# A block of attention values in front of the x0 projections, in the first two quarters of a Hyena and neighbourhood-attention layer

## The chip, the cores and the metric

The kernel runs on one core of one Trainium2 chip. The metric is the time of one execution on the device in microseconds (us), as the median of several runs. The kernel is one program without loops at run time: every loop below is unrolled by Python when the program is written.

## The reference

The layer takes 640 tokens of width 1024: 128 prompt tokens and 512 latent tokens (an 8 x 64 grid). After an adaptive scale and shift, one wide projection gives everything else:

```
z = h @ w_in
hy, g_h, qkv, g_a, m = split(z)          # 3*1024, 1024, 3*1024, 1024, 2*1024
hy = short_conv(hy, conv_w, conv_b)      # three taps along the sequence
v_h, x1, x0 = split(hy)
u = v_h * x1
y_h = (irfft(rfft(u, 2L) * rfft(filter, 2L)) + u * d_bias) * x0
y_a = attention(q, k, v)                 # 8 x 16 window plus context keys for the latents
p_h = (y_h * silu(g_h)) @ w_bh ;  p_a = (y_a * silu(g_a)) @ w_ba
out = (sigmoid(m_h) * p_h + sigmoid(m_a) * p_a) @ w_out
x  <- layer_norm(alpha * x + gate * out)
```

The new keys and values of the prompt are outputs too. All of it is float32; the kernel splits each operand into a high and a low part and multiplies three times (high by high, high by low, low by high).

## The kernel before

**Layout.** Channels lie on the 128 partitions, so a projection of 128 channels for 640 tokens is one "tile": eight steps of the contraction, three passes, two halves of 320 tokens, which makes 48 matmuls into two PSUM banks (`proj`, `accumulate`, L178 to L197). Two pools of four banks each share PSUM: `ps_mm` (`acc`, tag "mm") for projections and values, `ps_ax` (`aux`) for the rest.

**The Hyena branch** works in four quarters of 256 channels, two channel tiles each. For quarter q:

- `quarter_head(q)` (L503) projects the tiles 2q, 8+2q, 2q+1 and 9+2q. Each goes through `conv_tile` (L477): four copies on ACT (L482 to L486) bring the tile from PSUM into one of two buffers `zs`, which take turns; ACT makes the middle tap (L488), and DVE adds the two outer taps (two L490). The first of a pair is called u, the second x1, and DVE multiplies them (L513). Four buffers "u" and two buffers "cv" (for x1) take turns.
- `quarter_tail(q)` (L527) does the same with the tiles 16+2q and 17+2q, which are x0 and lie in the ring "yh" of nine rows. It ends with `gate_convs(q)`.
- `long_conv`, `long_conv_product` and `long_conv_back` are the long convolution: transposes (L547) and a Fourier transform of u on PE, products with the filter's spectrum on DVE (L588, L589, L591, L596, L597), and the way back (PE L171 to L173 and L648). `filter_spectrum(q)` makes that spectrum (PE L391 to L402, DVE L407, the products `fa`, `fb`, `fc`, `fd`). At the end DVE adds the bias term into u (L640, L650).
- `gate_conv(n)` (L520) multiplies u by x0 (L472, L475) and stores the product in DRAM from POOL's queue (L524). It is called twice for each n, from the tail and from the way back; the second call does the work, and with it u and x0 are free.

**The attention values** are computed by `values(m)` (L656), each call for 256 columns, in token-major form: the tokens are the stationary operand and the weights stream. One call takes two weight tiles. For each half of the contraction it writes 48 matmuls on the first four token tiles into two banks `v` (L669), then 12 on the fifth token tile into a third bank `ve` (L680). With a home given, as here, the result goes through two "cv" buffers (L689, L690) and is stored in DRAM by five transfers from SP's queue (L691 to L694).

**Weights.** `wtile` (L150) loads a raw tile on SP's queue, writes its negative into `wl` (ACT, L162), has POOL's queue add the tile from DRAM (L163) after ACT has made `wh` its copy in fp32r's precision (L164); there are two raw, two `wh` and three `wl` buffers.

**The order.** `quarters()` (L1324) strings heads, tails and values together as the main line. `convs()` and `filters()` are a side line; they wait for flags such as `whole1` (head 1 written) or `spectrum1`. `weave` (L1348) takes three steps of the side line for every two of the main line, and every second main step also takes one of `token_sums`. This sets the order in which instructions are written. In this stage the order of execution is then made by the framework's planner, which gives each engine, among what is ready, the instruction that was written first, going by estimated times; on each engine the chosen order is fixed in the program. The attention stage from L1399 on has its order written by hand.

```
    weave(chain(along(quarters(), sums, 2), hand_over()), braid(convs(), filters()), AHEAD_OF[0], AHEAD_OF[1])
```

Of the kernel before, what the change touches and what calls it, by code (L numbers as in the profile page):

```python
# [46 lines left out]
def tile_hyena_natten_step(ctx: ExitStack, tc: tile.TileContext, a, o):  # L47
# [50 lines left out]
    def acc(name):  # L98
        return ps_mm.tile([P, 512], F32, tag="mm", name=name)
# [6 lines left out]
    def row(pool, tag, name, dt=F32, bufs=NK + 1, n=NT):  # L106
        return pool.tile([P, NT + 4 if tag == "yh" else NT], dt, tag=tag, bufs=bufs, name=name)[:, :n]
# [42 lines left out]
    def wtile(i, eng=None, dst=None, width=P):  # L150
        if i in early:
            return early.pop(i)
        if i not in raws:
            wraw(i)
        if dst is None:
            wh = wp.tile([P, 1024], F32R, tag="wh", name=f"wh{i}")
            wl = wp.tile([P, 1024], F32R, tag="wl", bufs=3, name=f"wl{i}")
            dst = [wh[:]], [wl[:]]
        raw, n = raws.pop(i), 1024 // len(dst[0])
        if eng == "dma":  # L160
            (wh,), (wl,) = dst
            nc.scalar.activation(wl, raw[:], AF.Copy, scale=-1.0)  # L162
            nc.gpsimd.dma_start(wl, a["wall"][i], accum_op=ALU.add)  # L163
            nc.scalar.activation(wh, raw[:], AF.Copy)  # L164
        else:
            for j, (wh, wl) in enumerate(zip(*dst)):
                split(wh, wl, raw[:, n * j : n * j + n], eng)
        return [[w[c // n][:, c % n : c % n + width] for c in range(0, 1024, width)] for w in dst]
# [308 lines left out]
    def conv_tile(i, dst):  # L477
        lo, hi = yield from proj(i, eng="dma")
        convw = out["convw"]
        zs = zss[0]  # L480
        zss.reverse()
        nc.scalar.activation(zs[:, 1 : 1 + LP], lo[:, :LP], AF.Copy)  # L482
        nat = by_row(zs[:, GAP + 1 : NG + 1])
        nc.scalar.activation(nat[:, :, 7:8], from_blocks(lo[:, B7], 1), AF.Copy)
        nc.scalar.activation(nat[:, :, 0:2], from_blocks(lo[:, B01], 2), AF.Copy)  # L485
        nc.scalar.activation(nat[:, :, 2:7], from_blocks(hi[:, :HALF], 5), AF.Copy)  # L486
        d = dst[:, :NG]
        nc.scalar.activation(d, zs[:, 1 : 1 + NG], AF.Identity, scale=convw[:, i, 1:2], bias=convw[:, i, 3:4])  # L488
        for c in (0, 2):
            nc.vector.scalar_tensor_tensor(d, zs[:, c : c + NG], convw[:, i, c : c + 1], d, op0=ALU.mult, op1=ALU.add)  # L490
# [12 lines left out]
    def quarter_head(q):  # L503
        us = []
        out[f"u{q}"] = us
        for i in range(2):
            n = 2 * q + i
            u = hw.tile([P, NG + 1], F32, tag="u", bufs=4, name=f"u{n}")
            x1 = hwa.tile([P, NG + 1], F32, tag="cv", bufs=2, name=f"x1_{n}")
            yield from conv_tile(n, u)  # L510
            yield
            yield from conv_tile(8 + n, x1)
            nc.vector.tensor_tensor(u[:, :NG], u[:, :NG], x1[:, :NG], op=ALU.mult)  # L513
            us.append(u)
            yield
        out[f"whole{q}"] = True
# [10 lines left out]
    def quarter_tail(q):  # L527
        for i in range(2):
            n = 2 * q + i
            out["x0"][n] = row(yhp, "yh", f"x0_{n}", n=NG + 1)  # L530
            yield from conv_tile(16 + n, out["x0"][n])
            yield
        if q < 3:
            gate_convs(q)

    def gate_convs(q):
        for i in range(2):
            gate_conv(2 * q + i)
# [117 lines left out]
    def values(m, home=None):  # L656
        w = [wtile(T_V + 2 * m + i, "dma", width=256) for i in range(2)]
        ps = [acc(f"v{m}_{i}") for i in range(2)]

        def passes(k):  # L660
            wh, wl = w[k // 4][0][k % 4], w[k // 4][1][k % 4]
            return ((hH, wh, k == 0, False), (hL, wh, False, False), (hH, wl, False, k == NK - 1))

        for half in range(2):
            ks = range(4 * half, 4 * half + 4)
            for k in ks:
                for x, wk, first, last in passes(k):
                    for t in range(4):
                        nc.tensor.matmul(  # L669
                            ps[t // 2][:, t % 2 * 256 : t % 2 * 256 + 256], x[:, k, P * t : P * t + P], wk,  # L670
                            start=first and t % 2 == 0, stop=last, skip_group_check=True,
                        )
                yield
            if half:
                parts = [ps[0][:], ps[1][:]]
            else:
                pe = acc(f"ve{m}")
            for k in ks:
                for x, wk, first, last in passes(k):
                    nc.tensor.matmul(pe[:, :256], x[:, k, P * 4 :], wk, start=first, stop=last, skip_group_check=True)  # L680
            yield
        if home is None:
            v = out[f"v{m}"] = slot(m, "v", f"v{m}")
            for c, p in ((0, parts[0]), (512, parts[1]), (1024, pe[:, :256])):
                nc.scalar.activation(v[:, c : c + p.shape[-1]], p, AF.Copy)
        else:
            for i, p in enumerate(parts):
                v = hwa.tile([P, NG + 1], F32, tag="cv", bufs=2, name=f"v{m}_{i}")
                nc.scalar.activation(v[:, :512], p, AF.Copy)  # L689
                nc.scalar.activation(v[:, 512:640], pe[:, 128 * i : 128 * i + 128], AF.Copy)  # L690
                nc.sync.dma_start(home[m][:, 512 * i : 512 * i + 512], v[:, :512])  # L691
                nc.sync.dma_start(home[m][:, 1024 + 128 * i : 1152 + 128 * i], v[:, 512:640])
                if i == 0:
                    nc.sync.dma_start(o["new_v"][:, m * 256 : m * 256 + 256], v[:, :256])  # L694
            yield
            return
        nc.sync.dma_start(o["new_v"][:, m * 256 : m * 256 + 256], v[:, :256])
        yield
# [61 lines left out]
    def chain(*gens):  # L760
        for g in gens:
            yield from g
# [28 lines left out]
    def slot(j, tag, name, dt=F32):  # L791
        pool = out["slots_l" if j % 2 == 0 else "slots_q" if tag[0] == "q" else "slots_r"]
        return pool.tile([P, SLOT[tag]], dt, tag=tag, name=name)
# [529 lines left out]

    def quarters():  # L1324
        for q in range(3):
            yield from chain(quarter_head(q + 1), quarter_tail(q))
            if q < 2:
                yield from values(2 + q, v_d)

    def convs():  # L1330
        yield from chain(until("whole0"), long_conv(0))
        for q in range(4):
            yield from chain(until(f"spectrum{q}"), long_conv_product(q))
            back = long_conv_back(q)
            while f"rows{q}" not in out:
                yield next(back)
            if q < 3:
                yield from until(f"whole{q + 1}")
            yield from braid(back, long_conv(q + 1) if q < 3 else iter(()))
        yield from chain(until("slots_q"), attention_setup())  # L1340
# [5 lines left out]

    sums = chain(token_sums(0), token_sums(1))
    weave(chain(along(quarters(), sums, 2), hand_over()), braid(convs(), filters()), AHEAD_OF[0], AHEAD_OF[1])  # L1348
    out["slots_r"] = left.enter_context(tc.tile_pool(name="slots_r", bufs=1, reuse_waits="tile"))
    pinned[0] = True  # L1350
# [384 lines left out]
```

## Time and profile before

| | |
|---|---|
| median of 3 runs | 883.93 us (883.04 to 885.12) |
| profiled execution | 883.7 us, its span 881.9 us |
| PE busy | 866.0 us, 98% of the span |
| DVE busy | 645.1 us, 73% |
| ACT busy | 450.2 us, 51% |
| POOL busy | 189.0 us, 21% |
| DMA | 168.82 MB, 191 GB/s on average |

PE is the matmul engine (TensorE), PEld its weight loads, DVE the vector engine, ACT the scalar engine, POOL GpSimd, SP the queue that issues most transfers. A timeline row gives the start, the duration, the engine, the line of the kernel, the instruction with its output and inputs by name (buffer numbers left out), and in brackets how long the engine had been idle before and what released it. Rows that are merged carry a count at their end. A busy PE overlaps its matmuls: the time that one adds is the distance between starts, not its duration.

By the timeline the stages are: the prologue to about 50 us; the four quarters with values(2) at 111 to 128 us, values(3) at 197 to 219 and values(1) and values(0) at 296 to 329; queries, keys and the first gates to 358; the attention stage to about 702; the merge and the output to the end.

### The profile page before, as it was taken

To read this page: it belongs to the slowest core of one execution; us is meant where nothing else is said; L and a number is where in the kernel's file an instruction comes from. 1 tells how busy PE (TensorE), PEld (TensorE's weight loads), DVE (VectorE), ACT (ScalarE), POOL (GpSimd) and SP (SyncE) were. 2 spreads that over 40 slices of the span, in tenths; PEclk is the share of its full clock that TensorE was granted. 3 is DMA by queue.
4 is the path that set the end of the run, shared out by engine and by line. 5 is a ranking of instruction groups with operands and counts; after the bars stand their busy time and mean duration, and the time that the engine had idled before them with its cause. 6 is when DMAs were issued, how large, how long until landed. Compare 5 with 4: busy or idle time off the path is not lost.

```text
span 881.9 us, 17167 instructions
## 1 busy us (share of the span) xinstructions
PE 866.0 (98%) x6464; PEld 836.8 (95%) x6464; DVE 645.1 (73%) x1229; ACT 450.2 (51%) x960; POOL 189.0 (21%) x216
## 2 busy tenths in 40 slices
PE   8999999989999999999999999999999999999996
PEld 7899999979999999999999999999999999999885
DVE  4778986596895852787867787677778488667666
ACT  4396555546446453566566556656666532243200
POOL 0012210100100112084353334333454200000000
PEclk9999999989999999999999999999999999999999
DMA  8978886435664799978776668675854587445521
GB/s 326 400 170 226 231 215 145 92 103 138 162 132 96 202 228 241 308 218 252 172 238 164 220 153 260 138 212 158 232 138 120 180 301 246 160 165 187 183 88 56
DMA packets 75822, 168.82 MB, mean 191 GB/s; under 512 B 11067, under 2 KB 29243, under 8 KB 75740
## 3 DMA queue, kind: packets, MB, share of 16 engines
q1 hardware_dynamic: 56492, 123.32, 41.9%
q0 software_dynamic: 13632, 38.80, 22.8%
q10 hardware_dynamic: 5616, 5.61, 1.9%
q8 instruction: 51, 0.84, 0.4%
q14 instruction: 31, 0.25, 0.1%
HBM read 143.06 MB, written 23.99 MB: 189 GB/s over the span
## 4 chain that ended last, share of the span: by engine, by line
PE 94%; DVE 3%; DMA 1%; ACT 1%; issue 1%; SPq 0%; POOL 0%; POOLq 0%; DVEq 0%; ACTq 0%
PE mm L183 33%; PE sp L1238 30%; PE out L1545 6%; PE v L669 5%; PE s L1044 2%; PE s L951 2%; PE pt L1035 2%; PE ve L680 1%; DMA t<-tok_d 1%; PE adaT L253 1%; PE adaT L270 1%; PE yb L171 1%; PE yb L173 1%; PE yb L172 1%; PE ut L547 1%
## 5 line engine op out<-in xcount | busy, mean ns | idle before, releaser
L1238 PE MATMUL sp<-t,wb 128*128 128x320 f32 x1056 | 166.3, 311 | 0.4 <-DMA t<-tok_d 0.4
L1238 PEld LDWEIGHTS sp<-t,wb 128*128 128x128 f32 x1056 | 157.1, 188 | 1.2 <-DMA t<-tok_d 0.6
L1238 PE MATMUL sp<-hH,wb 128*128 128x320 f32 x524 | 126.4, 312 | 0.0
L1238 PEld LDWEIGHTS sp<-hH,wb 128*128 128x128 f32 x524 | 90.0, 188 | 2.6 <-issue 2.6
L163 POOL DMA_DIRECT2D wl<-wall x32 | 28.4, 889 | 248.2 <-ACT wl L162 212.5
L1238 PE MATMUL sp<-hL,wb 128*128 128x320 f32 x262 | 81.0, 309 | 0.0
L183 PE MATMUL mm<-hH,wh 128*128 128x320 f32 x312 | 77.6, 315 | 0.9 <-ACT hH L329 0.6
L183 PE MATMUL mm<-hH,wl 128*128 128x320 f32 x312 | 75.0, 312 | 0.4 <-DVE wl L103 0.4
L183 PE MATMUL mm<-hL,wh 128*128 128x320 f32 x312 | 74.7, 311 | 0.0
L1199 DVE TENSOR_TENSOR wb<-s,wb 128x512 fp32r<-128x512 f32 x66 | 47.1, 715 | 23.3 <-ACT wb L1191 23.2
L164 ACT ACTIVATE wh<-raw 128x1024 fp32r<-128x1024 f32 x32 | 34.0, 1061 | 58.9 <-PE mm L183 49.5
L1191 ACT ACTIVATE wb<-s 128x512 fp32r<-128x512 f32 x66 | 41.6, 632 | 37.8 <-PE sp L1238 19.1
L1006 POOL TENSOR_SCALAR edge<-edge,sm 128x320 f32<-128x320 f32 x32 | 43.1, 1526 | 66.6 <-DVE sm L1004 66.6
L183 PEld LDWEIGHTS mm<-hH,wh 128*128 128x128 f32 x312 | 53.6, 190 | 2.9 <-ACT zs L485 0.9
L1006 POOL TENSOR_SCALAR p<-p,sm 128x384 f32<-128x384 f32 x32 | 50.9, 1675 | 25.3 <-PE sp L1238 11.4
L183 PEld LDWEIGHTS mm<-hH,wl 128*128 128x128 f32 x312 | 53.1, 189 | 1.2 <-DVE wl L103 0.9
L183 PEld LDWEIGHTS mm<-hL,wh 128*128 128x128 f32 x312 | 53.1, 189 | 0.7 <-DVE hL L330 0.5
L1238 PEld LDWEIGHTS sp<-hL,wb 128*128 128x128 f32 x262 | 49.3, 188 | 0.0
L1545 PE MATMUL out<-woh,yhs 128*128 128x512 f32 (+1 forms) x176 | 45.5, 372 | 0.0
L1226 DVE TENSOR_TENSOR spare_hHp<-sp,yu 128x320 f32<-128x320 f32 x66 | 32.0, 484 | 17.3 <-PE sp L1238 11.8
L183 PE MATMUL mm<-yhs,wh 128*128 128x320 f32 x224 | 42.5, 309 | 0.0
L102 ACT ACTIVATE wh<-raw 128x1024 fp32r<-128x1024 f32 x15 | 15.8, 1058 | 46.9 <-PE mm L183 38.7
(414 smaller groups left out, 2269.1 us busy)
## 6 DMA issues: line engine op xcount, KB each, us to landing
raw<-wall SPq DMA_DIRECT2D x52, 512.0 KB, 3.8
wl<-wall POOLq DMA_DIRECT2D x32, 512.0 KB, 6.7
ra<-wall SPq DMA_DIRECT2D x22, 512.0 KB, 4.2
rb<-wall SPq DMA_DIRECT2D x42, 256.0 KB, 5.1
ada<-wada SPq DMA_DIRECT2D x16, 512.0 KB, 8.2
tm<-bias SPq DMA_DIRECT2D x16, 512.0 KB, 8.6
s<-wall SPq DMA_DIRECT2D x22, 256.0 KB, 4.5
s<-wall POOLq DMA_DIRECT2D x22, 256.0 KB, 4.4
```

The lines of the kernel that those rows point to most:

```text
L163: nc.gpsimd.dma_start(wl, a["wall"][i], accum_op=ALU.add)
L164: nc.scalar.activation(wh, raw[:], AF.Copy)
L183: nc.tensor.matmul(ps[hf][:, :HALF], wt[k], x[:, hf * HALF : (hf + 1) * HALF], start=(i == 0 and k == 0), stop=(i == lead[2] and k == NK - ...
L669: nc.tensor.matmul(ps[t // 2][:, t % 2 * 256 : t % 2 * 256 + 256], x[:, k, P * t : P * t + P], wk, start=first and t % 2 == 0, stop=last, ...
L951: nc.tensor.matmul(dst[h], x[rows(h), qs], y[rows(h), ks], start=i == 0, stop=i == 2, skip_group_check=True)
L1006: nc.gpsimd.tensor_scalar_mul(pv, pv, sm[:, 2, c : c + 1])
L1035: nc.tensor.transpose(pt[:, i * P : i * P + P], ps[h][:, c : c + P], ident)
L1191: nc.scalar.activation(made[g][:, 0], block(g), AF.Copy)
L1199: nc.vector.tensor_tensor(made[g][:, 1], block(g), f(made[g][:, 0]), op=ALU.subtract)
L1226: nc.vector.tensor_tensor(c, dst, c if j == 3 else ps["u"], op=ALU.add)
L1238: nc.tensor.matmul(dst, wk, x(xi, k), start=j < 4 and k == 0 and i == 0, stop=k == 3 and i == 2, skip_group_check=True,)
L1545: ins = nc.tensor.matmul(dst, m[k][:, c0 : c0 + P], w[:, c : c + n], start=(first and k == 0), stop=(last and k == 5), skip_group_check=True,)
```

## The change

In the main line the head and the tail of a quarter are no longer chained directly. Behind `quarter_head(1)` now stands `values(2)`, and then `quarter_tail(0)`; behind `quarter_head(2)` stands `values(3)`, and then `quarter_tail(1)`. The third turn has no values and stays as it was. Nothing else is edited.

```diff
     def quarters():
         for q in range(3):
-            yield from chain(quarter_head(q + 1), quarter_tail(q))
+            yield from quarter_head(q + 1)
             if q < 2:
                 yield from values(2 + q, v_d)
+            yield from quarter_tail(q)
```

## The prediction

> **What bounds the kernel now.** The page's busy times come first: TensorE (PE) is busy for 98% of the span, so a reordering can only win what PE loses somewhere, or lose more.
>
> ```profile
> PE 866.0 (98%) x6464; PEld 836.8 (95%) x6464; DVE 645.1 (73%) x1229; ACT 450.2 (51%) x960; POOL 189.0 (21%) x216
> ```
>
> Next, the table of stretches: length, then busy time of PE, weight loads, DVE, ACT and POOL, the granted clock, DMA share and GB/s. In the stage that the diff touches (about 60 to 350 us) PE is full everywhere but here:
>
> ```profile
> 100.00:120.00 20.00, 20.00 (x153) 19.82 (x153) 19.15 (x29) 10.66 (x21) 4.53 (x7) 1.00 0.84 246
> 176.00:180.00 4.00, 3.23 (x22) 2.87 (x20) 4.00 (x7) 1.02 (x2) 0.57 (x1) 1.00 0.77 247
> 180.00:184.00 4.00, 0.85 (x5) 0.65 (x5) 4.00 (x4) 1.99 (x4) 0.89 (x1) 0.79 0.71 162
> 184.00:188.00 4.00, 3.63 (x11) 2.91 (x12) 4.00 (x6) 1.99 (x6) 0.00 (x0) 0.50 0.67 140
> 188.00:192.00 4.00, 4.00 (x27) 4.00 (x26) 4.00 (x6) 0.63 (x1) 0.00 (x0) 0.85 0.12 33
> ...
> 180.00:200.00 20.00, 16.48 (x99) 15.38 (x100) 20.00 (x27) 9.57 (x22) 0.95 (x2) 0.83 0.37 82
> ```
>
> The hole costs 0.77 + 3.15 + 0.37 = 4.29 us of idleness, and then the clock is down: 0.85 x 0.21 + 3.63 x 0.50 + 4.00 x 0.15 = 2.6 us. Together 6.9 us; DVE is full all through it. The first row shows that in the first quarter, the other place of the change, PE has nothing to win.
>
> Why PE stops, from the timeline of PE:
>
> ```profile
> 171.44 0.31 PE L183 MATMUL mm<-hH,wh 128*128 128x320 f32 x1
> 178.78 0.46 PE L183 MATMUL mm<-hH,wl 128*128 128x320 f32 x2
> 180.22 0.39 PE L172 MATMUL fa<-sl,dftH 128*128 128x256 f32 x1 [0.99 <-DVE sl L103]
> 184.22 0.58 PE L171 MATMUL fb<-sh,dftH 128*128 128x256 f32 x1 [3.15 <-ACT sh L102]
> 185.80 0.63 PE L183 MATMUL mm<-hH,wh 128*128 128x320 f32 x1 [0.15 <-ACT zs L485]
> ```
>
> Projection tile 18 (x0 of head 2, the first tile of the second quarter's tail) runs from 171.44 to 179.24. After it only filter work (fa, fb) is at hand, and that hangs on DVE. Tile 19 begins at 185.80, the moment ACT has copied two PSUM banks out (L485). There are four banks for projections and a tile takes two: at 179.24 two hold tile 18, the other two tile 5 (u5). Who holds u5 up, on ACT and then DVE:
>
> ```profile
> 137.56 0.26 ACT L482 ACTIVATE zs<-mm 128x128 f32<-128x128 f32 x1
> 149.55 0.94 ACT L488 ACTIVATE x<-zs,pack 128x641 f32<-128x641 f32 x1
> 170.24 0.26 ACT L482 ACTIVATE zs<-mm 128x128 f32<-128x128 f32 x1
> 173.22 0.95 ACT L488 ACTIVATE u<-zs,pack 128x641 f32<-128x641 f32 x1
> 183.53 0.63 ACT L102 ACTIVATE sh<-sd 128x512 fp32r<-128x512 f32 x1
> 185.19 0.28 ACT L482 ACTIVATE zs<-mm 128x128 f32<-128x128 f32 x1 [1.02 <-DVE u L490]
> 185.46 0.29 ACT L485 ACTIVATE zs<-mm 128x128 f32<-128x128 f32 x1
> ```
>
> ```profile
> 171.96 0.78 DVE L475 TENSOR_TENSOR yu<-x,u 128x64 f32<-128x64 f32 x2
> 174.30 1.53 DVE L588 TENSOR_TENSOR W<-X,F 128x1280 f32<-128x1280 f32 x1
> 178.63 0.93 DVE L490 SCALAR_TENSOR_TENSOR u<-zs,pack,u 128x641 f32<-128x641 f32 x1
> 180.03 2.87 DVE L591 TENSOR_TENSOR X<-X,F 128x2560 f32<-128x2560 f32 x1
> 184.16 0.93 DVE L490 SCALAR_TENSOR_TENSOR u<-zs,pack,u 128x641 f32<-128x641 f32 x1
> 186.97 0.87 DVE L513 TENSOR_TENSOR u<-u,x 128x641 f32<-128x641 f32 x1
> 193.58 0.93 DVE L490 SCALAR_TENSOR_TENSOR u<-zs,pack,u 128x641 f32<-128x641 f32 x1
> 198.58 0.87 DVE L513 TENSOR_TENSOR u<-u,x 128x641 f32<-128x641 f32 x1
> ```
>
> Read backwards: tile 5 leaves PSUM at 185.19, when u4's second L490 frees the first of two zs buffers. Tile 4 had sat in that buffer since 137.56, because its next step (L488, 173.22) needs one of four u buffers, and u0 comes free only with its last product, L475 at 171.96. x1_4, written after u4, passed it at 149.55 (it needs no u): the planner lets what is ready pass what is blocked. So **PSUM banks full of tiles that wait for u0** bound PE here, and x0 tiles, which need zs and DVE too, are the wrong filler.
>
> **The change part by part.** No instruction is added or removed; weights, loads and stores are the same in number. Counted in yields, values take 11 and a tail 16, so outside the two swapped stretches the side generators stand at the same points as before.
>
> *The second quarter.* After x1_5 (copied out from 170.24) come values(3) instead of tile 18. They need neither zs nor DVE, and only two banks for the first 96 matmuls (both halves of the contraction for four token tiles); the remaining 24, on the fifth token tile, need a third. Cost of one matmul, from the chain's pieces:
>
> ```profile
> 304.24 5.76 PE v L669 x48
> 335.48 16.00 PE mm L183 x109
> ```
>
> That is 0.120 us for values and 0.147 for projections. Tile 18 filled 48 x 0.147 = 7.05 us; values fill 96 x 0.120 = 11.52, 4.47 more. Work thus reaches 179.24 + 4.47 = 183.71. The five fa matmuls of the hole follow (181.07 - 180.22 = 0.85) and fb with the next filter tile (some 0.6 at full clock): 185.16. Their input sh, done at 184.16, is there in time. The third bank is free at 185.46 + 0.29 = 185.75. **0.6 us of idleness remain of 6.9**, and no slow clock.
>
> If the planner held to the written order, the 12 matmuls that need the third bank would stand before the second half: 48 x 0.120 = 5.76 us of filler, 1.3 less than tile 18 gave, and the hole would grow to 8.2. That is one bound; I take the other end, because of x1_4's passing at 149.55.
>
> The rule of the Trainium skill, "TensorE: Matmul & The Clock Gate", section "What's actually happening", is that an idle window of about 3.4 us halves the PE clock until as long a busy stretch has passed. The trace agrees (0.50 granted behind idle times of 0.99 and 3.15 us). By that rule a rest of 0.6 us costs no clock, and the sum stays at its value; were the slow clock of the rows above to come all the same, it would be 2.6 us worse.
>
> ```profile
> 158.74 1.06 ACT L164 ACTIVATE wh<-raw 128x1024 fp32r<-128x1024 f32 x1 [0.62 <-PE mm L183]
> 196.86 1.06 ACT L164 ACTIVATE wh<-raw 128x1024 fp32r<-128x1024 f32 x1 [0.40 <-PE mm L183]
> ```
>
> *New waits.* values(3) leave through two "cv" buffers, which x1_4 and x1_5 hold until the products L513 at 186.97 and 198.58; before, both had long been free. So half of the values sits in two banks until 199.5, and tile 18, which runs with the other two, must be copied out before tile 19 can start. The 24 remaining matmuls take 2.9 us from 185.75, tile 18 then 7.05, with some 2.4 us of filter work between (tile 19 took from 185.80 to 196.86, where the next cast is released: 11.1 less 7.05 and 1.6 of slow clock): 198.1. Its zs buffer is free (u5's second L490 ends at 194.5), and a bank is out 0.6 us after the copy starts: **0.7 us of wait**; bounds 0 (filter work stands there) and 2.0 (the v copies come first, at 200.1). Behind the waiting copy on ACT's queue stand weight casts, on SP's queue behind the five stores of values stand loads of weights and decays. Tile 18's weights were cast at 158.74 for a start at 171.44, so 12 us of other tiles hide both; were that cover gone, one cast would cost 1.06 us. POOL's queue keeps its weight additions in a new order, and its yu stores sit behind the same products.
>
> *The first quarter.* Values(2) now run where tail(0) ran, and x0_0 and x0_1 come last:
>
> ```profile
> 114.53 1.77 ACT L488 ACTIVATE x<-zs,pack 128x641 f32<-128x641 f32 x2
> 117.72 1.68 DVE L490 SCALAR_TENSOR_TENSOR x<-zs,pack,x 128x641 f32<-128x641 f32 x2
> 119.92 2.81 DVE L591 TENSOR_TENSOR X<-X,F 128x2560 f32<-128x2560 f32 x1
> 122.65 1.68 DVE L490 SCALAR_TENSOR_TENSOR x<-zs,pack,x 128x641 f32<-128x641 f32 x2
> ```
>
> PE is full either way. Four L490 leave the path of L591, from which the long chain to u0's release starts: between 1.7 us earlier (the pair ahead of L591) and 1.7 later (all four now fall into the filter chain behind it). I take 0, since both are DVE time moved, not made.
>
> *u0's release.* The tail now ends after the side generators have written the next quarter's W and X products (L588, L591); the products L475 that free u0 are written with the tail's end, so they lose their place in the order. At 171.96 L475 stood in front of L588 at 174.30, whose input was not yet ready, and u4's L490, written later still, gets in at 178.63 before L591. I take 0 delay; the other end is the third rival below.
>
> *Downstream.* PE reaches the attention stage some 5 us earlier:
>
> ```profile
> 335.19 2.21 DVE L650 SCALAR_TENSOR_TENSOR u<-u,hyd,y 128x512 f32<-128x512 f32 x2 [7.55 <-PE y L648]
> 368.99 1.00 PE L1238 MATMUL sp<-t,wb 128*128 128x320 f32 x5 [0.41 <-DMA t<-tok_d]
> ```
>
> The last long convolution waits for PE (7.55), so it comes along; but PE already waits 0.41 us there for a load, and a shift not shared by all transfers lengthens that. Bounds 0 and the whole gain; I take 0.6, nearer to the row.
>
> **Sum**, against the profiled execution's 883.7 us (span 881.9): 883.7 - 6.9 + 0.6 + 0.7 + 0.6 = 878.7. The median of the runs shown is 883.93, 0.2 above it, so I predict 878.9.
>
> **Rivals.**
>
> 1. *The gain is eaten.* The filler works, but the transfers of the attention stage do not move, and the 0.41 us wait grows by what was won; or PE keeps the written order at the third bank (8.2 - 6.9 = 1.3 us worse). Against it: L650 waits for PE; x1_4 passed. 883.9, between 882.5 and 885.3. Chance 0.16.
>
> 2. *It doesn't do what it says.* The planner orders by readiness, and tile 18 could slip in front of the values again. Against it: the values' weights are now asked for first, and weights are made in the written order. 883.9. Chance 0.06.
>
> 3. *Slower: u0 is freed late.* L475 falls behind L588, its twin, L591 and the filter's small steps, which fill DVE from 174.30 to 182.90; u0 is then free at about 183 instead of 172.7, and tile 5 leaves PSUM up to 10 us later. The filler runs out at 185.2 all the same. With a delay d the hole is 0.6 + d and, once past about 3 us, 2.6 of slow clock: it decides from d = 3.4 (0.6 + 3.4 + 2.6 + 0.7 + 0.6 = 7.9 against 6.9). At d = 5 it is 886.5, at 10 it is 891.5. For it: DVE has no idle time from 180 to 200. Against it: the gaps of dependent steps let later work in, as at 178.63. Chance 0.20, at 886.5.
>
> **How the numbers follow.** Forecast 0.58, rivals 0.16, 0.06, 0.20. A measurement here tells 0.2%, 1.8 us, from no change: below 882.1 is faster, above 885.7 slower. Faster is the forecast and a little of the first rival, 0.60; the same is the rest of the first, the second and the mild end of the third, 0.22; slower 0.18. The range begins at 876.5, the whole hole gone and the load's 0.41 too (883.9 - 6.9 - 0.4 = 876.6), and reaches to 887, past the third rival at d = 5. The forecast's own range is 876.5 to 881.5.
>
> **What would show it.** Right: values(3) right behind x1_5 in PE's order, 96 of them before the matmuls on the fifth token tile; no idleness over 1 us and a granted clock of 1.00 between 176 and 192 us; x0's L488 and L490 after 200. Wrong in the size: a wait on t before 370 us, or a copy of v that waits for L513 with PE idle. Wrong altogether: L475 for u0 behind L588 and L591, u4's L488 later than 176, or a new hole at the change from one quarter to the next, where u6 waits for u2.

## The result, and the profile after

| | before | after |
|---|---|---|
| median of 5 runs | 884.04 us (883.04 to 885.12) | 878.90 us (877.56 to 880.31) |
| profiled execution, its span | 883.7, 881.9 us | 878.07, 876.3 us |

The ratio is 0.9944 (95% interval 0.9933 to 0.9955): faster by 0.56%, 5.1 us. The forecast was 878.9.

The table of stretches of the changed kernel, with the columns that the prediction explained:

```profile
176.00:180.00 4.00, 4.00 (x34) 3.91 (x33) 4.00 (x7) 0.00 (x0) 0.56 (x1) 1.00 0.74 240
180.00:184.00 4.00, 4.00 (x36) 4.00 (x34) 4.00 (x4) 0.41 (x1) 0.00 (x0) 1.00 0.02 8
184.00:188.00 4.00, 3.38 (x24) 2.74 (x23) 4.00 (x6) 3.17 (x8) 0.00 (x0) 1.00 0.11 37
188.00:192.00 4.00, 4.00 (x32) 4.00 (x31) 4.00 (x6) 3.48 (x6) 0.89 (x1) 1.00 0.67 176
...
196.00:200.00 4.00, 3.13 (x23) 2.83 (x23) 3.97 (x7) 0.91 (x5) 0.00 (x0) 1.00 1.06 278
```

PE is now idle for 0.62 us where the hole was and for 0.87 us some 14 us later (before 199.74), and the granted clock (third figure from the end) stays at 1.00. DVE is as full as before (4.00 of 4.00): what was taken from PE's way is not DVE's load.

The timeline of PE of the changed kernel, the first and last rows of the values and the first of the two tiles, with the waits:

```profile
171.43 0.40 PE L669 MATMUL v<-wh,hH 128*128 128x256 f32 x2
183.63 0.64 PE L669 MATMUL v<-wl,hH 128*128 128x256 f32 x4
184.76 0.38 PE L171 MATMUL fb<-sh,dftH 128*128 128x256 f32 x1 [0.50 <-ACT sh L102]
185.73 0.39 PE L680 MATMUL ve<-wh,hH 128*128 128x256 f32 x1
188.60 0.28 PE L680 MATMUL ve<-wl,hH 128*128 128x256 f32 x1
189.31 0.31 PE L183 MATMUL mm<-hH,wh 128*128 128x320 f32 x1
199.74 0.41 PE L183 MATMUL mm<-hH,wh 128*128 128x320 f32 x1 [0.86 <-ACT v L689]
```

Values(3) start right behind tile 13 (x1_5, the head's last) at 171.43, and all 96 matmuls on the first four token tiles run until 184.3, before the 24 on the fifth (`ve`, 185.73 to 188.72). Tile 18 follows at 189.31 and tile 19 at 199.74.

ACT of the changed kernel, and then DVE:

```profile
173.21 0.95 ACT L488 ACTIVATE u<-zs,pack 128x641 f32<-128x641 f32 x1
184.09 0.62 ACT L102 ACTIVATE sh<-sd 128x512 fp32r<-128x512 f32 x1
185.12 0.28 ACT L482 ACTIVATE zs<-mm 128x128 f32<-128x128 f32 x1 [0.41 <-DVE u L490]
185.40 0.29 ACT L485 ACTIVATE zs<-mm 128x128 f32<-128x128 f32 x1
189.80 0.57 ACT L689 ACTIVATE v<-v 128x512 f32<-128x512 f32 x1
199.09 0.60 ACT L689 ACTIVATE v<-v 128x512 f32<-128x512 f32 x1 [5.76 <-DMA v_d<-v]
```

```profile
115.61 2.82 DVE L591 TENSOR_TENSOR X<-X,F 128x2560 f32<-128x2560 f32 x1
171.94 0.75 DVE L475 TENSOR_TENSOR yu<-x,u 128x64 f32<-128x64 f32 x2
174.28 1.48 DVE L588 TENSOR_TENSOR W<-X,F 128x1280 f32<-128x1280 f32 x1
199.16 0.81 DVE L513 TENSOR_TENSOR u<-u,x 128x641 f32<-128x641 f32 x1
```

The product that frees u0 (L475) runs at 171.94, against 171.96 before; u4's L488 at 173.21, against 173.22; tile 5 leaves PSUM at 185.12, against 185.19. **Nothing of the chain that held tile 5 has moved; PE has other work while it lasts.**

The books of the two profiled executions: the span is 5.6 us shorter. The hole has to be priced anew first. By microsecond, the kernel before shows:

```profile
181.00:182.00 1.00, 0.07 (x1) 0.00 (x0) 1.00 (x1) 0.00 (x0) 0.72 (x1) 1.00 0.81 147
182.00:183.00 1.00, 0.00 (x0) 0.00 (x0) 1.00 (x2) 0.01 (x1) 0.18 (x1) 0.68 0.89 360
```

The granted clock was full until about 182.4, so the 0.85 us of work from 180.22 on ran at full speed, and the slow clock cost 2.4 us and not 2.6. The hole of 4.3 + 2.4 = 6.7 us is replaced by 0.62 + 0.87 us, and the wait of 0.41 us on t is gone: 6.7 - 1.5 + 0.4 = 5.6.

### The profile page after: what moved, and what is told of

It is laid out like the page before. It is cut to its first block, busy times and chain, and to the rows that moved or that the text cites. A ratio compares the mean times of both kernels' runs of the same rounds, so it can differ in the third digit from the quotient of the medians.

```text
span 876.3 us, 17158 instructions
## 1 busy us (share of the span) xinstructions
PE 863.6 (99%) x6464; PEld 834.9 (95%) x6464; DVE 645.4 (74%) x1229; ACT 448.4 (51%) x960; POOL 188.7 (22%) x216
## 4 chain that ended last, share of the span: by engine, by line
PE 95%; DVE 3%; ACT 1%; DMA 1%; issue 0%; POOL 0%; POOLq 0%; SPq 0%; ACTq 0%
PE mm L183 34%; PE sp L1238 31%; PE out L1546 6%; PE v L669 4%; PE s L1044 3%; PE s L951 2%; PE pt L1035 2%; PE ve L680 1%; PE adaT L253 1%; DMA v_d<-v 1%; PE adaT L270 1%; PE yb L171 1%; PE yb L173 1%; PE yb L172 1%; PE ut L547 1%; PE mm1lo L183 0%
## 5 line engine op out<-in xcount | busy, mean ns | idle before, releaser
L183 PE MATMUL mm<-hH,wh 128*128 128x320 f32 x312 | 74.8, 312 | 1.6 <-ACT v L689 0.9
```

The lines of the kernel that those rows point to most:

```text
L183: nc.tensor.matmul(ps[hf][:, :HALF], wt[k], x[:, hf * HALF : (hf + 1) * HALF], start=(i == 0 and k == 0), stop=(i == lead[2] and k == NK - ...
```

## The experiments

All times are medians; each ratio is to the kernel before, measured alongside on the same chip (883.77 to 884.19 us).

### Each quarter alone

The second quarter alone:

```diff
         for q in range(3):
-            yield from chain(quarter_head(q + 1), quarter_tail(q))
-            if q < 2:
+            yield from quarter_head(q + 1)
+            if q == 1:
+                yield from values(2 + q, v_d)
+            yield from quarter_tail(q)
+            if q == 0:
                 yield from values(2 + q, v_d)
```

> The new order in the second quarter alone: values(3) in front of tail(1); in the first quarter tail(0) stays in front of values(2). Bank theory (the prediction's): all of the gain lies in the hole at 176 to 192 us of the kernel before, which belongs to the second quarter; so the whole gain of 5.1 us is there, 878.5 to 879.3, and PE's idle time between 176 and 204 us is that of the changed kernel, 0.5 + 0.5 + 0.9 us with a granted clock of 1.00. Rival (both quarters share in it, since x0's DVE work is moved out of two busy stretches): about half of the gain, 881 to 882.

The first quarter alone is the same with the two numbers of q exchanged.

> The new order in the first quarter alone: values(2) in front of tail(0); the second quarter as before. Bank theory: PE is full in the first quarter in either order, so nothing: 883.4 to 884.6, with the hole of 4.3 us idle time and the slow clock at 176 to 192 us in its place. Rival (x0's L490 leaving the way of the filter products L591 shifts the chain to u0's release): the hole shrinks by the 1.7 us of the prediction's bound or more, 880 to 882.

Second quarter alone: 879.77 us, ratio 0.9950 (0.9936 to 0.9964). First quarter alone: 884.51 us, ratio 1.0005 (0.9996 to 1.0014). **The gain belongs to the second quarter**; the first gives nothing that can be told from zero. The stretches of the first quarter alone show the hole as it was:

```profile
180.00:184.00 4.00, 0.85 (x5) 0.64 (x5) 4.00 (x4) 2.03 (x3) 0.90 (x1) 1.00 0.70 221
184.00:188.00 4.00, 2.98 (x9) 2.26 (x10) 4.00 (x6) 2.64 (x7) 0.00 (x0) 0.52 0.81 147
188.00:192.00 4.00, 4.00 (x20) 4.00 (x20) 4.00 (x6) 0.63 (x1) 0.00 (x0) 0.63 0.14 41
```

The second quarter alone lies 0.5 us above the range that I gave for it. Its waits of PE (total, times, longest) show where that profiled execution lost more than the changed kernel's, which has neither of these two rows:

```profile
PE sp L1238 <- DMA t<-tok_d: 1.7, 1, 1.7
PE yb L171 <- ACT ph L102: 0.5, 1, 0.5
```

So the wait on t, 0.41 us before, is 0 with both quarters changed and 1.7 with one. These rows make 2.2 of the 2.8 us by which its span is longer; its wait on tile 19 is 0.6 shorter, and its first projection starts 0.7 later in the prologue (11.69 against 11.04), so about 0.5 us stays unexplained. The intervals of the two overlap, and whether the first quarter's order has a part in the wait on t stays open.

### Tile 18 first, then values, then tile 19

```diff
-    def quarter_tail(q):
+    def quarter_tail(q, between=None):
...
             yield from conv_tile(16 + n, out["x0"][n])
             yield
+            if i == 0 and between is not None:
+                yield from between
...
-            yield from chain(quarter_head(q + 1), quarter_tail(q))
-            if q < 2:
-                yield from values(2 + q, v_d)
+            yield from chain(quarter_head(q + 1), quarter_tail(q, values(3, v_d) if q == 1 else None))
+            if q == 0:
+                yield from values(2, v_d)
```

> The second quarter as tile 18, then values(3), then tile 19; the first quarter as before. Bank theory: at about 179 us two of the four projection banks hold tile 18 and two hold tile 5, so the values that are written next get no bank and PE stops as before: idle time near 4 us and a slow clock between 176 and 192 us, 883 to 885. Rival (the gain comes from moving x0's L488 and L490 out of the stretch where DVE is full): tile 19's share of it is moved, so half of the gain or more, 881 to 882.

885.22 us, ratio 1.0008 (0.9999 to 1.0016): nothing gained. PE in that kernel:

```profile
184.85 0.58 PE L171 MATMUL fb<-sh,dftH 128*128 128x256 f32 x1 [3.14 <-ACT sh L102]
186.44 0.80 PE L671 MATMUL v<-wh,hH 128*128 128x256 f32 x2 [0.15 <-ACT zs L485]
```

The values need no zs and no DVE, and yet they wait for L485, tile 5's copy out of PSUM, as tile 19 did before. **It is banks that PE lacks**; values help only where they are the first to take the two free ones.

### u4 without its wait

The kernel before in its old order, u4 alone in a row of the "yh" ring instead of the u ring:

```diff
-            u = hw.tile([P, NG + 1], F32, tag="u", bufs=4, name=f"u{n}")
+            if n == 4:
+                u = row(yhp, "yh", "u4", n=NG + 1)
+            else:
+                u = hw.tile([P, NG + 1], F32, tag="u", bufs=4, name=f"u{n}")
```

> The kernel before in its old order, with u4 alone put into a free row of another buffer, so that it waits for no u buffer. Theory (the hole is tile 4 waiting for u0, which keeps a zs buffer from tile 5): u4's L488 runs some 30 us earlier, near 140 us, tile 5 leaves PSUM by about 160 us, and the hole of 6.9 us goes: 877 to 879. Rival (DVE, which has no idle time in the hole, is what bounds PE there): the same DVE work stands in the same stretch, the hole keeps at least half of its length, 881 to 884.

878.15 us, ratio 0.9930 (0.9918 to 0.9943): 6.0 us without the change under study. ACT and one stretch:

```profile
162.92 0.93 ACT L488 ACTIVATE u<-zs,pack 128x641 f32<-128x641 f32 x1
165.79 0.28 ACT L482 ACTIVATE zs<-mm 128x128 f32<-128x128 f32 x1 [1.94 <-DVE u L490]
```

```profile
180.00:184.00 4.00, 4.00 (x28) 3.91 (x27) 4.00 (x4) 1.57 (x2) 0.89 (x1) 1.00 0.72 205
```

u4 is made at 162.92, not near 140 as I expected (what holds it until then is not shown), but that is early enough: tile 5 leaves at 165.79 instead of 185.19, and PE is full. DVE is full in that stretch too, so a full DVE as such doesn't stop PE. The same edit on top of the change:

> The changed kernel with u4 in a free row of another buffer, so that it waits for no u buffer. Theory: what PE still loses there in the changed kernel (0.5 us on fb behind sh, 0.9 us on tile 19 behind the copy of v) goes with it, since tile 5 leaves PSUM some 25 us earlier and x1_4's buffer is free sooner: 877.0 to 878.0. Rival (with tile 4 out of the way there is always a bank, so the order of values and x0 tiles no longer matters and the time is that of the old order with u4 in its row, measured at 878.15): 877.8 to 878.6.

877.99 us, ratio 0.9938 (0.9926 to 0.9949). In its profile PE has no idle time from 168 to 224 us, so both remaining waits are gone. Its interval and those of the changed kernel and of the run before overlap: no order of the three can be given, and a version that surely beats the change was not found. A fifth u buffer, the plainest cure, was not tried.

### The written order at the third bank

```diff
                     for t in range(4):
+                        with tc.issue_after(fifth) if half and m == 3 else nullcontext():
...
-                    nc.tensor.matmul(pe[:, :256], x[:, k, P * 4 :], wk, start=first, stop=last, skip_group_check=True)
+                    fifth = nc.tensor.matmul(pe[:, :256], x[:, k, P * 4 :], wk, start=first, stop=last, skip_group_check=True).ins
```

> The changed kernel, with the second half of the contraction of values(3) for the first four token tiles (48 matmuls) made to run behind the matmuls on the fifth token tile, which need a third bank: the order as it is written, with no passing. Theory (the prediction's bound): the filler is 5.76 us instead of 11.52, the hole grows from 0.6 to about 8.2 us with the slow clock in it, 1.3 us more than in the kernel before: 884.5 to 886.5. Rival (the passing is not what makes the gain; tile 18 or filter work fills the place): 878 to 881.

885.67 us, ratio 1.0022 (1.0013 to 1.0032): slower than before. Its stretches:

```profile
176.00:180.00 4.00, 2.92 (x23) 2.48 (x21) 4.00 (x7) 0.02 (x1) 0.57 (x1) 1.00 0.79 211
180.00:184.00 4.00, 1.31 (x5) 1.02 (x5) 4.00 (x4) 0.09 (x1) 0.00 (x0) 0.66 0.20 82
184.00:188.00 4.00, 2.71 (x9) 1.99 (x10) 4.00 (x6) 2.90 (x7) 0.00 (x0) 0.50 0.12 33
188.00:192.00 4.00, 4.00 (x22) 4.00 (x22) 4.00 (x7) 2.52 (x3) 0.00 (x0) 0.56 0.24 47
```

Idle 1.08 + 2.69 + 1.29 = 5.1 us, and by the mean clock of each row 0.34 x 1.31 + 0.50 x 2.71 + 0.44 x 4.00 = 3.6: a hole of 8.6 us where the bound said 8.2. **The gain needs the second half of the contraction to pass the matmuls that wait for the third bank**; without it the change costs 1.9 us.

### u0 freed late

Maxima of u0 with itself (in place, the values stay) just ahead of the product that frees it; here six, in others one or two:

```diff
+            if n == 0:
+                for _ in range(6):
+                    nc.vector.tensor_tensor(us[0][:, :NG], us[0][:, :NG], us[0][:, :NG], op=ALU.max)
             gate_conv(n)
```

> The changed kernel with six maxima of u0 with itself on DVE (some 0.8 us each, 4.9 us in all; they change no value) just ahead of the product that frees u0: the delay d of the prediction's third rival, put in by hand. Theory (the third rival's price): a hole of 0.6 + d and 2.6 us of slow clock, 885 to 887.5. Rival (planner and filter work close it, or the wait of 0.9 us on tile 19 is only moved): 879 to 882.

> The kernel before with the same six maxima ahead of the product that frees u0. Theory (u0's release sets the hole): the hole of 4.3 us idle time grows by the delay, 4.9 us, and the clock is already slow there, so 888 to 890. Rival (the hole hangs on fb's input sh and on DVE as a whole, which has slack behind it): 884 to 886.

898.09 us on the changed kernel and 902.85 on the kernel before: both far past every figure given, since the maxima did not run together. DVE of the changed kernel with six (the first, the second, and the product for u0):

```profile
172.51 0.82 DVE L655 TENSOR_TENSOR u<-u 128x641 f32<-128x641 f32 x1
174.91 1.47 DVE L588 TENSOR_TENSOR W<-X,F 128x1280 f32<-128x1280 f32 x1
177.71 0.81 DVE L655 TENSOR_TENSOR u<-u 128x641 f32<-128x641 f32 x1
199.67 0.74 DVE L475 TENSOR_TENSOR yu<-x,u 128x64 f32<-128x64 f32 x2
```

Each maximum needs the one before it, and in between the planner's order has the filter's products (L588 here). 4.9 us of work became a delay of 27 us. So the same with one and two:

> The changed kernel with one maximum of u0 with itself ahead of the product that frees u0 (0.8 us of DVE work; with six of them the product came 27.5 us later and the kernel 19.2 us slower than the changed one). If the product keeps its place, it moves by the 0.7 us that the maximum adds to DVE, and the time is 879 to 880.5. If it loses its place to the filter's products L588 and L589, as the second of the six did, it comes at about 177.7 us, d = 5.7: then the prediction's price (0.6 + d of hole, 2.6 of slow clock) gives 878.9 + 5.7 + 2.6 = 887.2, and the rate of the six maxima (19.2 / 27.5 = 0.70 us for each us of delay) gives 882.9.

> The changed kernel with two such maxima. Where the six stood, the third came at 183.2 us; the product in its place is d = 11.3 us late. The prediction's price gives 878.9 + 11.3 + 2.6 = 892.8; the rate of the six gives 886.8; a product that keeps its place gives 880 to 881.

> The kernel before with one such maximum. The hole is there already and the clock slow in it, so a product at 177.7 us costs the whole d = 5.7 by the price of the hole (889.8), 4.0 by the rate of the six (888.0), and 0.7 where it keeps its place (884.8).

ACT in the changed kernel with one maximum, then with two, then in the kernel before with one; in each u4's L488 and the start of tile 5's copy:

```profile
178.42 0.93 ACT L488 ACTIVATE u<-zs,pack 128x641 f32<-128x641 f32 x1 [3.04 <-DVE yu L475]
188.56 0.28 ACT L482 ACTIVATE zs<-mm 128x128 f32<-128x128 f32 x1 [3.22 <-DVE u L490]
```

```profile
184.12 0.92 ACT L488 ACTIVATE u<-zs,pack 128x641 f32<-128x641 f32 x1
192.19 0.28 ACT L482 ACTIVATE zs<-mm 128x128 f32<-128x128 f32 x1 [3.36 <-DVE u L490]
```

```profile
178.33 0.93 ACT L488 ACTIVATE u<-zs,pack 128x641 f32<-128x641 f32 x1 [3.04 <-DVE yu L475]
188.45 0.28 ACT L482 ACTIVATE zs<-mm 128x128 f32<-128x128 f32 x1 [3.82 <-DVE u L490]
```

| kernel | u4's L488 later by | tile 5 out later by | time | longer by |
|---|---|---|---|---|
| before, one | 5.1 | 3.3 | 887.24 | 3.4 |
| before, six | 26.9 | 21.7 | 902.85 | 19.1 |
| changed, one | 5.2 | 3.4 | 884.40 | 5.5 |
| changed, two | 10.9 | 7.1 | 885.23 | 6.3 |
| changed, six | 27.2 | 22.7 | 898.09 | 19.2 |

The kernel before is measured against itself alongside, the changed one against 878.90. With one maximum u0's product came at 177.6, as expected for a lost place, but all three times of the kernels with one and two maxima miss the figures given: 884.40 lies between the two prices (882.9 and 887.2), 885.23 and 887.24 lie below both.

**The time is nearer to the shift of tile 5's copy out of PSUM than to the delay of u0**: with one maximum 5.2 us of delay move the copy by 3.4, because u4's two L490 follow at 183.95 and 187.55, 3.6 us apart instead of 5.5. In the kernel before the time grows by about that shift (3.4 for 3.3, 19.1 for 21.7). In the changed one with one maximum it grows by more. There, PE's idle time between 184 and 192 us grows by 2.3 only (0.62 to 2.92), since filter work fills a part; the slow clock adds 1.7 and a later wait on sh (at 204.57) 1.6, and the wait of 0.87 on tile 19 is gone. That is 4.7 of the 6.0 us between the two profiled executions; the rest was not followed. One maximum takes away the whole gain (ratio to the kernel before 1.0014, 1.0005 to 1.0023): it hangs on u0's product not being 5 us later.

### The second wait

The second half of values(3) copied into a row of the "yh" ring instead of a "cv" buffer:

```diff
-                v = hwa.tile([P, NG + 1], F32, tag="cv", bufs=2, name=f"v{m}_{i}")
+                if m == 3 and i == 1:
+                    v = row(yhp, "yh", "v3_1", n=NG + 1)
+                else:
+                    v = hwa.tile([P, NG + 1], F32, tag="cv", bufs=2, name=f"v{m}_{i}")
```

> The changed kernel, with the second half of values(3) copied out into a free row of another buffer instead of a cv buffer. By the trace of the changed kernel its copy L689 waits till 199.09 us for the store of the first half from the same buffer, and tile 19 waits 0.9 us for that copy. Theory: the copy runs right behind the first half's, before 195 us, and the 0.9 us go: 877.5 to 878.5. Rival (the copy waits for its PSUM data or ACT, or tile 19 waits for tile 18's own copy anyway): the wait on tile 19 stays at 0.5 us or more, 878.5 to 879.5.

879.70 us, ratio 0.9956 (0.9944 to 0.9969): no gain over the change. The copy no longer waits (ACT, L692 is the edit's L689), but PE does, for something else:

```profile
191.02 0.58 ACT L692 ACTIVATE v<-v 128x512 f32<-128x512 f32 x1
```

```profile
199.63 0.57 PE L183 MATMUL mm<-hH,wl 128*128 128x320 f32 x2 [1.09 <-DMA wl<-wall]
```

The copy theory held for the copy and failed for the time: tile 19 now waits for the addition to its weights. POOL issued it at 189.95, and at 189.67 in the changed kernel. The table of transfers (line, number, size, us from issue to landing) gives, here and then in the changed kernel:

```profile
wl<-wall POOLq DMA_DIRECT2D x1, 512.0 KB, 9.6
```

```profile
wl<-wall POOLq DMA_DIRECT2D x1, 512.0 KB, 6.7
```

So it landed at 199.55 here and at 196.4 in the changed kernel, 3.3 us before tile 19 began: this wait came with the edit. What made it slower stays open; stores of values leave beside it in both kernels (from 190.40 in the changed one, from 191.62 here).

## Why the prediction was right, point by point

- **The bound.** Right. Only the second quarter gives anything, banks are what is missing (tile 18 first gives nothing), and u4's buffer is the cause (u4 in another row gives all).
- **The hole, 6.9 to 0.6 us.** Measured 6.7 to 0.62 us, and no slow clock is left. In the 6.9 the first term, 0.85 x 0.21, was misread: those matmuls ran before the clock fell. In the 0.6 the split was different: the input sh of fb was to be "there in time" and came 0.50 us late (fb at 184.76), and the third bank, which was to cost it all, cost about 0.1: the matmuls on the fifth token tile start at 185.73, right behind L485's end at 185.40 + 0.29 = 185.69. So the wait for sh hid nearly all of the wait for the bank. The sum came out the same because both ends held: the same work stood ahead of the bank, and tile 5's copy had not moved.
- **The planner passes what is blocked.** Right, and it decides the sign: 8.6 us of hole and 885.67 us without it, against the bound of 8.2.
- **The new wait, 0.7 us (0 to 2.0).** 0.86 us measured, but for another reason, so the near hit is luck. I had the second half of the values wait for L513 at 198.58 and tile 19 for tile 18's copy. In the trace the copy starts at 199.09, before L513 at 199.16, released by the store of the first half, which left SP's queue at 190.4 to 193.1; tile 19 waits for this copy. That the weights stay hidden held for tile 19 (its addition landed at 196.4), but not where the copy of v was moved.
- **The first quarter, 0.** Right in time (ratio 1.0005), wrong in the reason: L591 moved by 4.3 us (119.92 to 115.61), beyond the bound of 1.7, and u0's product still ran at 171.94. So an earlier L591 doesn't bring u0's release forward, and the chain that the prediction let start there is not what sets it.
- **u0's release, 0 delay.** Right: 171.94, ahead of L588 at 174.28.
- **Downstream, 0.6 us.** Too much for the profiled execution: the wait on t is gone. The timeline of SP's queue, before and then after, shows the loads of t moving with PE:

```profile
355.45 1.97 SPq L64 DMA_DIRECT2D t<-tok_d  x4
```

```profile
350.75 2.71 SPq L64 DMA_DIRECT2D t<-tok_d  x4
```

They are issued 4.7 us earlier. That refutes the first rival's reason (transfers that don't move) for this execution. The wait itself was 0, 0.2, 0.4 and 1.7 us in kernels that differ only 150 us earlier, so 0.6 was a guess within a spread that the rows of the kernel before could not narrow.

- **The sum.** With the measured terms, 883.7 - 6.7 + 0.62 + 0.87 - 0.41 = 878.1, against 878.07 for the profiled execution. The forecast of 878.9 had 0.6 for downstream that this execution didn't need. That it is the median to the last digit is luck: the five runs lie between 877.56 and 880.31.
- **Rivals.** The second fell with the order in PE's timeline. The third did not happen, but the mechanism is real: with one dependent step more, the product came 5.7 us later and u4's L488 5.2. Its price was too high: 886.5 at d = 5, where 884.40 was measured. The failing step is "with a delay d the hole is 0.6 + d": tile 5's copy moved by 3.4 only, and the idle time of the hole grew by 2.3. Its slow clock did come. By its own sum the third rival was level with the kernel before at d = 2.4 (0.6 + 2.4 + 2.6 + 0.7 + 0.6 = 6.9), not at 3.4.

## What to carry to other kernels

When PE stops while DVE is full, ask who holds the PSUM banks and read back from the copy that frees them to the buffer that it waits for; then either give that buffer elsewhere or put work there that needs none of the missing resources, and count its banks. A reorder by which blocked work is passed is worth what the planner can pass: find out which part of the filler needs one bank more. Before taking a wait away, ask what the earlier work will start: here a copy that came 8 us sooner took away a wait of 0.9 us and came with one of 1.1, on a transfer that took 9.6 us instead of 6.7.

## What the runs showed of the hardware

The clock falls on idle time that is split up, not only on an unbroken stretch. In the changed kernel with one maximum PE idles 0.85, 1.47 and 0.60 us between 184.5 and 189.2, with work between; then the granted clock is down for 3.4 us though PE is full. By microsecond:

```profile
189.00:190.00 1.00, 0.83 (x6) 0.83 (x7) 1.00 (x2) 1.00 (x4) 0.00 (x0) 0.95 0.00 0
190.00:191.00 1.00, 1.00 (x7) 1.00 (x6) 1.00 (x3) 0.77 (x1) 0.00 (x0) 0.50 0.52 148
...
193.00:194.00 1.00, 1.00 (x8) 0.92 (x7) 1.00 (x3) 1.00 (x2) 0.00 (x0) 0.84 0.91 330
```

A single wait of 1.09 us (values in a row) or of 0.86 (the changed kernel) cost no clock. The time at half clock, added up from rows of 1 us, comes in steps: 3.4 us here (0.1 + 3 + 0.3), 6.8 in the kernel before, with the first quarter alone, and in the changed kernel with two maxima, 10.2 with the written order and in the kernel before with one maximum. These are one, two and three times 3.4 us, and the full clock does not come back as soon as the waits end: in the kernel before, the last wait of the hole ended at 185.8, and the clock came back at 189.2.

The Trainium skill, "TensorE: Matmul & The Clock Gate", Part 1, has the clock set by how busy PE was in a free-running window of about 3.4 us; the fall after 2.9 us of idleness in pieces and the steps of 3.4 us agree with that. The prediction's "an idle window" with "the trace agrees" was too narrow a reading: in the kernel before, too, the clock fell at 182.4, 1.3 us into the wait of 3.15 us, and no unbroken idle stretch reached 3.4.
